# Eight experts on one core: the last result in a used buffer, stored by one DMA

## The chip, the cores and the metric

The kernel runs on 1 core of one Trainium2 chip. The time is device microseconds for the whole program, as the median of the runs. The profile is of one more execution with its own time; its span runs from the first to the last instruction, and all positions below are microseconds from the start of that span.

## The reference

For each of 8 experts there are 256 rows of 512 inputs, and two weight matrices. Everything comes in and goes out as 32-bit floats.

```
x (8, 256, 512)   w1 (8, 512, 2048)   w2 (8, 2048, 512)   b1 (8, 2048)   b2 (8, 512)
h   = max(x @ w1 + b1, 0)
out = h @ w2 + b2            # (8, 256, 512)
```

The weights of one expert are 4 MB each for w1 and w2, so the 8 experts read 64 MB of weights in all. One result is 512 KB.

## The kernel before

One expert is one stage. In stage s the kernel does the first product of expert s and the second product of expert s - 3 (`LAG = 3`), so there are 11 stages. TensorE transposes x (`transposes`, L101), makes 16 blocks of the hidden layer by 64 matmuls (`first_product`, L114), and for the second product adds the bias by a one-row matmul (L156) and then accumulates 32 matmuls into two PSUM tiles of 128 x 512 (`second_product`, L162). ScalarE applies the bias and the rectifier (L121).

The loads are issued by GpSimd, since they turn 32-bit floats into 16-bit ones on the way. They stand in a list called `ring`, whose order is fixed by hand: x and w1 of expert s, w2 of expert s - 3. `second_product` of the last expert reads its w2 from three pieces (`load_w2_piece`, L92), so that it can begin on the first. Those pieces are the last loads of the list.

The results of experts 0 to 6 are not stored when they are ready. `store` copies the two PSUM tiles into an SBUF tile `out`, one half by VectorE (L139) and one by ScalarE (L140), and remembers the tile in `pending`. `flush` (L135) issues the stores from GpSimd, behind all loads. The list ends with these flushes in the order of the experts, so the seven results lie in one DMA queue behind the last weights. Expert 5's result is stored in three parts by partition (`PARTS`): 25 partitions by SyncE (L145), 96 and 7 by GpSimd.

The result of expert 7 does not go into the list. VectorE copies one half, and SyncE stores that half (L148, 256 KB); ScalarE copies the other half and stores it itself (L149, 256 KB).

The tiles called `out` come from a pool of 8 buffers that go round. The first two hold the 32-bit x of experts 0 and 1 at the start, so the results of experts 0 to 5 take the other six buffers, and the results of experts 6 and 7 take the first two again. Those had been free since the first microseconds.

Of the kernel before, what the change touches and what calls it, by code (L numbers as in the profile page):

```python
# [11 lines left out]
def kernel(  # L12
# [9 lines left out]
    nc = tc.nc  # L22
    fp32 = mybir.dt.float32
    fp16 = mybir.dt.float16
    E, T, H = x.shape
    M = w1.shape[2]
    P = 128
    nTB = T // P
    nKC = H // P
    nJ = M // P  # L30
    LAG = 3
    LATE = range(E - 1)

    PARTS = {5: ((0, 25, True), (25, 121, False), (121, 128, False))}
# [9 lines left out]
    x_pool = ctx.enter_context(tc.tile_pool(name="xp", bufs=4))  # L46
    xT_pool = ctx.enter_context(tc.tile_pool(name="xTp", bufs=2))
    hT_pool = ctx.enter_context(tc.tile_pool(name="hT", bufs=LAG + 1))
    out_pool = ctx.enter_context(tc.tile_pool(name="outp", bufs=E))
    psum_x = ctx.enter_context(tc.tile_pool(name="psum_x", bufs=1, space=bass.MemoryType.PSUM))  # L50
    psum_h = ctx.enter_context(tc.tile_pool(name="psum_h", bufs=3, space=bass.MemoryType.PSUM))
    psum_o = ctx.enter_context(tc.tile_pool(name="psum_o", bufs=2, space=bass.MemoryType.PSUM))
# [10 lines left out]
    w1_sb = [None] * E  # L63
    w2_sb = [None] * E
    hT = [None] * E
    pending = {}

    def load_x(e):
# [66 lines left out]
                ordered(nc.gpsimd.dma_start(out=dst[p0:p1], in_=src[p0:p1]))  # L135

    def store(e, po):
        out_sb = out_pool.tile([P, nTB, H], fp32, tag="out", name="out")
        nc.vector.tensor_copy(out=out_sb[:, 0, :], in_=po[0])  # L139
        nc.scalar.copy(out=out_sb[:, 1, :], in_=po[1])  # L140
        dst = out[e].rearrange("(p tb) h -> p tb h", tb=nTB)
        if e < E - 1:
            for p0, p1, sync in PARTS.get(e, ()):
                if sync:
                    nc.sync.dma_start(out=dst[p0:p1], in_=out_sb[p0:p1])  # L145
            pending[e] = (dst, out_sb)
        else:
            nc.sync.dma_start(out=dst[:, 0, :], in_=out_sb[:, 0, :])  # L148
            nc.scalar.dma_start(out=dst[:, 1, :], in_=out_sb[:, 1, :])  # L149

    def second_product(e):
        po = []
        for tb in range(nTB):
            t = psum_o.tile([P, H], fp32, tag=f"po{tb}", name=f"po{tb}")
            po.append(t)
            ordered(nc.tensor.matmul(  # L156
                out=t, lhsT=ones1, rhs=b2_sb[0:1, e * H : (e + 1) * H], start=True, stop=False,
            ))
        for lo, hi, t in w2_sb[e]:
            for tb in range(nTB):  # L160
                for j in range(lo, hi):
                    ordered(nc.tensor.matmul(  # L162
                        out=po[tb],
                        lhsT=hT[e][:, j, tb * P : (tb + 1) * P],
                        rhs=t[:, j - lo, :],
                        start=False,
                        stop=(j == nJ - 1),
                    ))
        store(e, po)

    x32 = []
    for e in range(nXF32):
        x32.append(out_pool.tile([P, nTB, H], fp32, tag="out", name="x32"))
        (nc.sync if e == 0 else nc.scalar).dma_start(
            out=x32[e], max_dma_last_dim=2048, in_=x[e].rearrange("(p tb) h -> p tb h", tb=nTB)
# [4 lines left out]
        out=b2_sb,  # L180
        in_=b2.rearrange("e h -> (e h)").rearrange("(o f) -> o f", o=1),
# [10 lines left out]
    for j in range(nJ):  # L192
        for s in range(2):
            ordered(nc.tensor.matmul(  # L194
                out=pb[s * 64 : (s + 1) * 64, j, :, :],
# [5 lines left out]
    for s in range(2):  # L201
        nc.vector.tensor_copy(  # L202
            out=b1T[s * 64 : (s + 1) * 64, :, :], in_=pb[s * 64 : (s + 1) * 64, :, :, s]
# [13 lines left out]
    for lo, hi in ((0, 8), (8, 12), (12, 16)):  # L217
        ring.append((0, load_w2_piece, (E - 1, lo, hi)))
    for e in LATE:
        ring.append((e + LAG + 1, flush, (e,)))  # L220
# [40 lines left out]
```

## Time and profile before

| What | Value |
|---|---|
| median of 9 runs | 183.86 us (183.78 to 184.18) |
| the profiled execution's own time | 184.15 us |
| its span | 182.4 us |
| DMA, mean over the span | 222 GB/s on the SBUF side of the packets |
| HBM read and written | 71.39 MB and 4.19 MB, 414 GB/s over the span |
| TensorE busy | 135.7 us (74% of the span) |
| ScalarE busy | 62.6 us (34%) |
| GpSimd, VectorE busy | 20.1 us (11%), 13.2 us (7%) |

A load counts in the GB/s of the packets with the 16-bit size that arrives, so a stretch of loads at about 220 GB/s reads twice that from HBM. A stretch of stores moves 32-bit floats on both sides. The DMA row of the page gives the mean busy share of the core's 16 DMA engines in tenths for each of 40 slices of 4.56 us.

### The profile page before, as it was taken

To read this page: it belongs to the slowest core of one execution; us is meant where nothing else is said; L and a number is where in the kernel's file an instruction comes from. 1 tells how busy PE (TensorE), PEld (TensorE's weight loads), DVE (VectorE), ACT (ScalarE), POOL (GpSimd) and SP (SyncE) were. 2 spreads that over 40 slices of the span, in tenths; PEclk is the share of its full clock that TensorE was granted. 3 is DMA by queue.
4 is the path that set the end of the run, shared out by engine and by line. 5 is a ranking of instruction groups with operands and counts; after the bars stand their busy time and mean duration, and the time that the engine had idled before them with its cause. 6 is when DMAs were issued, how large, how long until landed. Compare 5 with 4: busy or idle time off the path is not lost.

```text
span 182.4 us, 2120 instructions
## 1 busy us (share of the span) xinstructions
PE 135.7 (74%) x912; PEld 94.6 (52%) x912; DVE 13.2 (7%) x21; ACT 62.6 (34%) x137; POOL 20.1 (11%) x43
## 2 busy tenths in 40 slices
PE   1805979479550999849980999849999999998700
PEld 1804979469540854845480754836489444433200
DVE  0410001001000101010100101010100101010100
ACT  0112679639560330924090330915059010100100
POOL 7200030300300010201010000200051011112100
PEclk9999999969998599999998599997999999999995
DMA  5999989998999999999999999999998999999992
GB/s 160 261 226 232 230 173 230 201 259 187 217 230 226 194 212 230 196 235 201 230 226 212 194 230 226 198 208 230 226 230 178 226 205 226 205 228 210 398 410 101
DMA packets 5687, 40.58 MB, mean 222 GB/s; under 512 B 654, under 2 KB 670, under 8 KB 3374
## 3 DMA queue, kind: packets, MB, share of 16 engines
q0 software_dynamic: 4784, 38.71, 96.3%
q1 hardware_dynamic: 446, 0.89, 1.4%
q10 hardware_dynamic: 448, 0.85, 1.4%
q8 instruction: 7, 0.11, 0.2%
q14 instruction: 2, 0.02, 0.0%
HBM read 71.39 MB, written 4.19 MB: 414 GB/s over the span
## 4 chain that ended last, share of the span: by engine, by line
DMA 68%; PE 24%; POOL 1%; issue 1%; ACT 0%; POOLq 0%
DMA x<-in_x_dram 44%; DMA w<-in_w_dram 16%; PE po L162 12%; PE ph L114 10%; DMA w1sb<-in_w_dram 8%; PE psx L101 1%; POOL w2sb L86 1%; PE po L156 1%; ACT out L140 0%; POOL w1sb L76 0%; POOLq L245 0%
## 5 line engine op out<-in xcount | busy, mean ns | idle before, releaser
L114 PE MATMUL ph<-xT,w1sb 128*128 128x256 f16 x512 | 67.7, 298 | 12.5 <-DMA w1sb<-in_w_dram 12.5
L121 ACT ACTIVATE hT<-ph,b1T 128x256 f16<-128x256 f32 x128 | 57.0, 474 | 44.6 <-PE ph L114 44.5
L114 PEld LDWEIGHTS <-w1sb 128*128 128x128 f16 x512 | 61.1, 148 | 18.3 <-DMA w1sb<-in_w_dram 13.4
L162 PE MATMUL po<-w2sb,hT 128*128 128x512 f16 x224 | 49.6, 379 | 0.0
L162 PEld LDWEIGHTS <-hT 128*128 128x128 f16 x256 | 24.5, 98 | 32.4 <-issue 4.1
L140 ACT COPY out<-po 128x512 f32<-128x512 f32 x8 | 4.7, 590 | 57.0 <-PE po L162 57.0
L101 PE MATMUL psx<-ident,x 128*128 128x128 f16 x64 | 6.2, 254 | 19.1 <-DMA x<-in_x_dram 18.4
L101 PEld LDWEIGHTS <-x 128*128 128x128 f16 x64 | 5.0, 124 | 20.1 <-DMA x<-in_x_dram 19.4
L76 POOL DMA_DIRECT2D w1sb<-in_w_dram x8 | 4.4, 555 | 64.9 <-PE ph L114 64.1
L107 DVE COPY xT<-psx 128x1024 f16<-128x1024 f16 x8 | 5.5, 692 | 83.3 <-PE psx L101 83.3
L86 POOL DMA_DIRECT2D w2sb<-in_w_dram x9 | 4.8, 536 | 55.3 <-PE po L162 55.3
L139 DVE COPY out<-po 128x512 f32<-128x512 f32 x8 | 5.5, 692 | 69.2 <-PE po L162 69.2
L162 PE MATMUL po<-w,hT 128*128 128x512 f16 x32 | 7.1, 379 | 0.7 <-DMA w<-in_w_dram 0.7
L135 POOL DMA_DIRECT2D out_dram<-out x8 | 4.3, 533 | 29.7 <-DVE out L139 8.7
L194 PE MATMUL pb<-ident,b_rows 16*64 16x16 f32 x64 | 3.7, 265 | 4.1 <-DMA b_rows<-in_b_dram 4.1
L194 PEld LDWEIGHTS pb<-ident,b_rows 16*64 16x64 f32 x64 | 3.6, 198 | 4.0 <-POOL ident masks.py:199 4.0
L156 PE MATMUL po<-b_sb,ones 1*128 1x512 f16 x16 | 4.8, 379 | 0.0
L121 ACT ACT_TABLE_LOAD x1 | 1.3, 1283 | 8.5 <-DVE b1T L202 8.5
L70 POOL DMA_DIRECT2D x<-in_x_dram x6 | 3.6, 598 | 0.7 <-DMA w1sb<-in_w_dram 0.7
L156 PEld LDWEIGHTS <-ones 1*128 1x128 f16 x16 | 0.9, 92 | 2.1 <-issue 2.1
L189 DVE CAST x<-x 128x1024 f16<-128x1024 f32 x2 | 1.4, 694 | 4.6 <-DMA x<-in_x_dram 4.6
L92 POOL DMA_DIRECT2D w<-in_w_dram x3 | 1.6, 557 | 0.0
(9 smaller groups left out, 2.6 us busy)
## 6 DMA issues: line engine op xcount, KB each, us to landing
w1sb<-in_w_dram POOLq DMA_DIRECT2D x8, 2048.0 KB, 33.8
w2sb<-in_w_dram POOLq DMA_DIRECT2D x5, 2048.0 KB, 46.6
w2sb<-in_w_dram POOLq DMA_DIRECT2D x4, 1024.0 KB, 28.0
out_dram<-out POOLq DMA_DIRECT2D x6, 512.0 KB, 21.1
x<-in_x_dram POOLq DMA_DIRECT2D x6, 256.0 KB, 39.3
w<-in_w_dram POOLq DMA_DIRECT2D x1, 1024.0 KB, 29.5
w<-in_w_dram POOLq DMA_DIRECT2D x2, 512.0 KB, 32.4
x<-in_x_dram SPq DMA_DIRECT2D x1, 512.0 KB, 4.2
```

The source lines that it names most:

```text
L76: ordered(nc.gpsimd.dma_start(out=w1_sb[e], in_=w1[e].rearrange("(p kc) m -> p kc m", kc=nKC)))
L86: ordered(nc.gpsimd.dma_start(out=t[:, lo : lo + step, :], in_=src[:, lo : lo + step, :]))
L101: ordered(nc.tensor.transpose(out=pt[:, kc, tb * P : (tb + 1) * P], in_=x16[e][:, tb, :].rearrange("p (q kc) -> p q kc", kc=nKC)[:, :, kc] ...
L107: nc.vector.tensor_copy(out=xT[e], in_=pt)
L114: ordered(nc.tensor.matmul(out=ph, lhsT=w1_sb[e][:, kc, :].rearrange("p (q j) -> p q j", j=nJ)[:, :, j], rhs=xT[e][:, kc, :], start=(kc == 0),
L121: nc.scalar.activation(out=hT[e][:, j, :], in_=ph, func=mybir.ActivationFunctionType.Relu, bias=b1T[:, j, e : e + 1], scale=1.0,)
L135: ordered(nc.gpsimd.dma_start(out=dst[p0:p1], in_=src[p0:p1]))
L139: nc.vector.tensor_copy(out=out_sb[:, 0, :], in_=po[0])
L140: nc.scalar.copy(out=out_sb[:, 1, :], in_=po[1])
L156: ordered(nc.tensor.matmul(out=t, lhsT=ones1, rhs=b2_sb[0:1, e * H : (e + 1) * H], start=True, stop=False,))
L162: ordered(nc.tensor.matmul(out=po[tb], lhsT=hT[e][:, j, tb * P : (tb + 1) * P], rhs=t[:, j - lo, :], start=False, stop=(j == nJ - 1),))
L194: ordered(nc.tensor.matmul(out=pb[s * 64 : (s + 1) * 64, j, :, :], lhsT=b1_rows.rearrange("r (q j) -> r q j", j=nJ)[:, :, j], rhs=ident[0 ...
```

## The change

The pool of `out` tiles has 7 buffers in place of 8. The results of experts 0 to 6 are kept in a list `results`, and expert 7's result goes into the tile of expert 4 (`REUSED = 4`). Its two copies therefore wait until the store of expert 4's result has been read out of that tile and has completed. The result is then stored by one SyncE DMA of 512 KB, and ScalarE issues no store. The positions of the first six results in the pool do not matter to anything else; experts 5 and 6 now take the two buffers that held x at the start.

```
-    out_pool = ctx.enter_context(tc.tile_pool(name="outp", bufs=E))
+    out_pool = ctx.enter_context(tc.tile_pool(name="outp", bufs=E - 1))
...
     def store(e, po):
-        out_sb = out_pool.tile([P, nTB, H], fp32, tag="out", name="out")
+        if e < E - 1:
+            results.append(out_pool.tile([P, nTB, H], fp32, tag="out", name="out"))
+        out_sb = results[e] if e < E - 1 else results[REUSED]
         nc.vector.tensor_copy(out=out_sb[:, 0, :], in_=po[0])
         nc.scalar.copy(out=out_sb[:, 1, :], in_=po[1])
         dst = out[e].rearrange("(p tb) h -> p tb h", tb=nTB)
-        if e < E - 1:
-            for p0, p1, sync in PARTS.get(e, ()):
-                if sync:
-                    nc.sync.dma_start(out=dst[p0:p1], in_=out_sb[p0:p1])
-            pending[e] = (dst, out_sb)
-        else:
-            nc.sync.dma_start(out=dst[:, 0, :], in_=out_sb[:, 0, :])
-            nc.scalar.dma_start(out=dst[:, 1, :], in_=out_sb[:, 1, :])
+        if e == E - 1:
+            nc.sync.dma_start(out=dst, in_=out_sb)
+            return
+        for p0, p1, sync in PARTS.get(e, ()):
+            if sync:
+                nc.sync.dma_start(out=dst[p0:p1], in_=out_sb[p0:p1])
+        pending[e] = (dst, out_sb)
```

No instruction changes its place on TensorE or GpSimd. On VectorE and ScalarE the last copy gains a wait on the DMA of expert 4's store. SyncE's last DMA is 128 x 1024 elements in place of 128 x 512 and waits for both copies; ScalarE's DMA behind its last copy is gone.

More of the change, by code (lines that the diff above doesn't have):

```diff
@@ L32 @@
     LATE = range(E - 1)
+    REUSED = 4
     PARTS = {5: ((0, 25, True), (25, 121, False), (121, 128, False))}
@@ L65 @@
     hT = [None] * E
+    results = []
     pending = {}
```

## The prediction

> **What bounds the kernel now.** I read the page's slices first, then the chain of waits, then the end of the span in finer windows.
>
> ```profile
> span 182.4 us, 2120 instructions
> ...
> DMA  5999989998999999999999999999998999999992
> GB/s 160 261 226 232 230 173 230 201 259 187 217 230 226 194 212 230 196 235 201 230 226 212 194 230 226 198 208 230 226 230 178 226 205 226 205 228 210 398 410 101
> ...
> q0 software_dynamic: 4784, 38.71, 96.3%
> ```
>
> The DMA engines are busy at nine tenths or more in nearly every slice, and 96.3% of that is GpSimd's queue q0. TensorE is busy for 74% and ends its last matmul at 172.1. From 169 on the rate stands near 400 GB/s: the loads are over and the stores drain. So the end is set by when the DMA engines have moved the last byte, and only the last 10 us are touched by the change. The chain of waits ends at the ScalarE copy (172.12 + 0.59) and does not follow the stores after it. The timeline of the end, and the times to landing, show what comes then:
>
> ```profile
> 160.58 0.53 POOL L135 DMA_DIRECT2D out_dram<-out  x1 [4.31 <-DMA w2sb<-in_w_dram]
> ...
> 170.47 0.55 POOL L135 DMA_DIRECT2D out_dram<-out  x1 [2.24 <-DMA w<-in_w_dram]
> 171.25 0.69 DVE L139 COPY out<-po 128x512 f32<-128x512 f32 x1 [8.51 <-PE po L162]
> 171.97 0.35 SPq L148 DMA_DIRECT2D out_dram<-out  x1
> 172.12 0.59 ACT L140 COPY out<-po 128x512 f32<-128x512 f32 x1 [7.75 <-PE po L162]
> 172.73 0.37 ACTq L149 DMA_DIRECT2D out_dram<-out  x1
> ```
>
> ```profile
> out_dram<-out SPq DMA_DIRECT2D x1, 256.0 KB, 6.6
> out_dram<-out ACTq DMA_DIRECT2D x1, 256.0 KB, 7.6
> ```
>
> The issue at 160.58 is expert 4's store (the fifth flush; asked for alone it lands 15.8 us later, at 176.4). The one at 170.47 is expert 6's; it lands after 9.6 us, at 180.1. Expert 7's halves land at 178.6 and 180.3. The last landing, 180.3, starts the end of the program, 2.1 us of waits and drains up to 182.4. Flushes 0 to 4 land some 1.3 us apart (30.0, 26.4, 22.9, 19.4 and 15.8 us after their issues at 141.16, 145.99, 150.84, 155.74 and 160.58), which is 512 KB at 419 GB/s.
>
> The DMA packets by queue, from 172 to 175.4, and the last stretches, with their DMA share and GB/s in the last two columns:
>
> ```profile
> DMA packets 384, 1.43 MB, mean 419 GB/s; under 512 B 37, under 2 KB 37, under 8 KB 383
> q0 software_dynamic: 383, 1.42, 101.9%
> q14 instruction: 1, 0.01, 0.6%
> ```
>
> ```profile
> 177.00:178.00 1.00, 0.00 (x0) 0.00 (x0) 0.00 (x0) 0.00 (x0) 0.00 (x0) 0.50 1.04 402
> 178.00:178.50 0.50, 0.00 (x0) 0.00 (x0) 0.00 (x0) 0.00 (x0) 0.00 (x0) 0.50 0.92 365
> 178.50:179.00 0.50, 0.00 (x0) 0.00 (x0) 0.00 (x0) 0.00 (x0) 0.00 (x0) 0.50 0.77 315
> 179.00:179.50 0.50, 0.00 (x0) 0.00 (x0) 0.00 (x0) 0.00 (x0) 0.00 (x0) 0.50 0.22 86
> 179.50:180.00 0.50, 0.00 (x0) 0.00 (x0) 0.00 (x0) 0.00 (x0) 0.00 (x0) 0.50 0.03 12
> ```
>
> The store issued by SyncE at 171.97 moves no packet up to 175.4: q1, SyncE's queue, is missing. Its first packet comes 3.5 us after the issue, and that of ScalarE's store 3.55 us after its own (packet records of the trace). The second block shows a ragged end. Adding up the shares from 178.0, all engines at full load would have ended at 178.97; a few run on to 179.77, and the last landing is 0.56 us behind that.
>
> **The change part by part.**
>
> *Removed: the early start.* Before, the halves are issued at 171.97 and 172.73. Now the copies wait for expert 4's landing. Nothing ahead of that landing changes in GpSimd's queue, and the SyncE packets began only at 175.47, so I leave it at 176.4. Had these packets held it up it would come some 0.2 us earlier: the nearest row against that is the spacing of 1.3 us from flush 3 to flush 4, as for the earlier ones. Waits on a DMA release TensorE here within 0.05 us (164.97 to 165.01).
>
> *Added: the wait.* VectorE's copy runs from 176.43 to 177.12 (0.69), ScalarE's beside it for 0.59. SyncE issues 0.03 later, as at 171.97 behind the copy's end at 171.94: 177.15. Behind the waiting copies nothing is queued: they are the last work of VectorE and ScalarE, and the DMA is SyncE's last. TensorE is done at 172.1, and the flushes of experts 5 and 6 are already issued at 165.56, 167.71 and 170.47. So the wait costs only what the late issue costs.
>
> *Moved: 512 KB behind the ring.* After flush 4 the ring holds 384 + 28 + 512 KB, 0.95 MB, which at 419 GB/s is 2.26 us. By bytes, the engines run dry of it at 178.97 - 1.25 = 177.7 on the mean. The latest one ends at 179.77 now; without its share of expert 7 (32 KB, eight packets of 4 KB, at an engine's 26 GB/s 1.25 us) at about 178.5. This is the cover: as long as the new store's packets are there by 177.7 to 178.5, the same bytes run through the same engines and nothing is lost.
>
> *How soon they are there* is the unknown. Bounds: at the start of the program, with the engines idle, the SyncE load of x at 0.74 has its first packet 1.08 us after its issue and ScalarE's load of b_rows 1.41 us. Under a full ring it is 3.5 us, as above. I take 1.3, since the ring is nearly empty when the store comes, and since ScalarE's second load at the start (x, issued at 1.22) began at 4.13, just as SyncE's was ending: a new queue seems to wait behind what the engines hold, and no longer. First packet 178.45; lowest 178.2, highest 180.65.
>
> The Trainium skill, "DMA: Bandwidth & Descriptors", section "Queues, rings and completion order", says that each engine goes round its queues packet by packet, so a new queue should not have to wait for another's ring to drain. The row disagrees: 2.2 to 2.4 us more than at the start, some fifteen 4 KB packets per engine. By the rule the latency would be the idle one, ring or not, and the likeliest sum below needs no luck; by the row alone it would be 3.5 us and the sum 186.0. I go with an explanation for both rows, a backlog that is gone at 178.
>
> *The transfer itself.* 512 KB at 419 GB/s is 1.25 us; the x load at the start took about 2.35 us from its first to its last packet, its first packets 0.6 us each. A store at the end of a draining ring is nearer to the stores, so I take 1.6. The landing comes 0.36 us (expert 6) to 0.56 us (expert 7) after the last packet; I take 0.5. Sum: 177.15 + 1.3 + 1.6 + 0.5 = 180.55, which is 3.4 us after issue. The x load as a whole, the one 512 KB DMA by SyncE in this trace, took 4.2 us.
>
> Against the change speaks a rule of the same page, section "Anatomy of one DMA — SWDGE (gpsimd) path": a DMA has a fixed part near 2.0 us, most of it the wait for the write to be confirmed (fitted for GpSimd's DMAs). Here it is paid twice in a row, for expert 4 and expert 7. The trace shows confirmations of 0.36 to 0.56 us, the first of which lies under the ring. The rule's 2.0 + 1.2 us would give an estimate of 180.35, hardly different from before; the rows give 180.55, and I keep them.
>
> *Edits at nothing.* ScalarE's DMA issue (0.37 us) goes away; at 172.73 it lay beside a drain of 7 us. Packets are 4 KB in place of 2 KB: from 176.2 to 178.1, with three queues mixed, the rate is 403 GB/s against 419, and 4% of 3 us is 0.12 us at most, a gain. One wait fewer stands at the end; these waits are under 0.03 us each. The smaller pool puts results 5 and 6 into buffers free since 7 us. If any of that cover is wrong the sizes stay under 0.2 us.
>
> *The sum.* The last landing goes from 180.3 to 180.55, +0.25 us on the span. The profiled execution took 184.15 (span 182.4 and 1.75 outside), 0.29 above the median, so I put the difference on the median: 183.86 + 0.25 = 184.1.
>
> **The rivals.**
>
> *The latency under load stays* (slower). Mechanism: the first packet of a SyncE store takes 3.5 us after its issue however little of the ring is left. Place: between 177.15 and 180.65, with the engines idle from 178.5. Then 180.65 + 1.25 + 0.5 = 182.4, +2.1, 186.0 us. It decides once the first packet is later than about 178.9. For it: all three hardware-queue stores here took 3.3 to 3.5 us, the 100 KB one at 156.85 too. Against it: the 1.08 and 1.41 us at the start.
>
> *The store starts cold* (slower). As the x load: 4.2 us from issue to landing, 181.35, +1.0, 184.9 us. For it: the only SyncE DMA of this size. Against it: that one read HBM with 64 KB of b_rows in between.
>
> *The drain becomes tidier* (faster). All engines start on the store with nothing else in the way: 1.08 + 1.25 + 0.36 from 177.15 is 179.85, -0.45, 183.4 us. For it: the ragged end, some 0.8 us in which most engines idle, and the 4% of mixed packets. Against it: the latest engine has the same bytes to move and ends near 179.7 anyway, so two things must go right.
>
> That the change does not do what it says I rule out: the copies could start at 171.25 and 172.12, and expert 4's store lands 4 us later, so the wait holds.
>
> **How the numbers follow.** A measurement of this kernel tells about 0.2%, 0.37 us, from no change: 183.49 to 184.23. The likeliest case, the overlap nearly complete, has 0.55, with its own range 183.6 to 184.55; of it 0.03 is faster, 0.36 the same and 0.16 slower. The cold start has 0.22 and the loaded latency 0.13, both slower. The tidier drain has 0.10, 0.09 faster and 0.01 the same. That makes faster 0.12, same 0.37, slower 0.51. Slower holds more than half, but split over three cases, so the predicted time is the likeliest case's, 184.1. The range 183.5 to 185.6 takes in that case, the cold start with 0.7 us beyond it and some of the tidier drain; it leaves out the loaded latency and the best of the faster case.
>
> **What would show it.** In the changed profile, VectorE's last copy should start near 176.4, released by a DMA, and SyncE's issue stand near 177.15. The first q1 packets are right at 178.2 to 178.6, wrong near 180. The DMA share should stay near 1 up to 177.5 and have at most a short dip before 179, no stretch of 1 us at nothing. The store should land 3.1 to 3.7 us after its issue. The prediction is wrong if that is over 4 us, or if expert 4's landing has moved by more than 0.3 us.

## The result: 0.65% faster, and the profile after

The changed kernel takes 182.69 us in the median of 10 runs (182.46 to 183.38), the kernel before 183.92 (31 runs, 183.77 to 184.24). The ratio is 0.9935, with a 95% interval of 0.9927 to 0.9943: 1.2 us faster. The forecast was 184.1 with a range of 183.5 to 185.6, so it had the wrong sign, and the measured time lies below the range.

The profiled execution took 182.66 us, with these lines on its page:

```profile
span 180.9 us, 2122 instructions
...
DMA  5999999999998999999999989999998999999995
GB/s 162 266 225 234 207 199 232 192 228 217 230 232 177 232 228 210 199 232 228 196 214 222 234 188 225 228 199 210 232 228 187 221 212 217 210 226 207 341 419 225
...
q0 software_dynamic: 4784, 38.71, 97.1%
```

The loads are as before, in bytes (q0's packets are the same) and in rate, near 220 GB/s. The difference is at the end. The timeline of the changed kernel:

```profile
170.51 0.55 POOL L137 DMA_DIRECT2D out_dram<-out  x1 [2.23 <-DMA w<-in_w_dram]
176.41 0.59 ACT L146 COPY out<-po 128x512 f32<-128x512 f32 x1 [11.45 <-DMA out_dram<-out]
176.43 0.69 DVE L145 COPY out<-po 128x512 f32<-128x512 f32 x1 [13.10 <-DMA out_dram<-out]
177.20 0.35 SPq L149 DMA_DIRECT2D out_dram<-out  x1
```

Up to SyncE's issue, things went as forecast: both copies are released by a DMA at 176.4, and SyncE issues at 177.20 (177.15 was forecast). After that it is quicker. The times to landing are these, first of SyncE's single store and then of expert 6's, the last that GpSimd issues:

```profile
out_dram<-out SPq DMA_DIRECT2D x1, 512.0 KB, 2.6
```

```profile
out_dram<-out POOLq DMA_DIRECT2D x1, 512.0 KB, 8.1
```

SyncE's store lands at 179.8 (before, the later half landed at 180.3). Expert 6's store is issued at the same time as before and lands at 178.6, where it was 180.1. The last stretches, with DMA share and GB/s at the right:

```profile
177.00:177.50 0.50, 0.00 (x0) 0.00 (x0) 0.12 (x1) 0.00 (x0) 0.00 (x0) 0.50 0.74 303
177.50:178.00 0.50, 0.00 (x0) 0.00 (x0) 0.00 (x0) 0.00 (x0) 0.00 (x0) 0.50 0.41 164
178.00:178.50 0.50, 0.00 (x0) 0.00 (x0) 0.00 (x0) 0.00 (x0) 0.00 (x0) 0.50 0.95 385
178.50:179.00 0.50, 0.00 (x0) 0.00 (x0) 0.00 (x0) 0.00 (x0) 0.00 (x0) 0.50 1.02 418
179.00:179.50 0.50, 0.00 (x0) 0.00 (x0) 0.00 (x0) 0.00 (x0) 0.00 (x0) 0.50 0.66 262
```

There is a dip between 177 and 178, in which the DMA engines run out of the ring's packets, and then SyncE's store almost alone. The dip costs 0.4 us of DMA time, and the kernel is faster all the same.

The last landing moved by 0.5 us and the span by 1.5. (The profiled execution of the kernel before was 0.2 us above its median, the changed one at its own; so the spans differ by somewhat more than the medians.) The other 1.0 us lies between the last landing and the end: 2.1 us before, 1.0 us now. What stands there are the closing instructions of the program. Among them are DRAINs: GpSimd stands at one for some 10 us here, until 1.5 us after its last DMA has landed. They are listed for the line that opens the kernel's context (count; duration in ns, least, median and longest; first and last start). Of the kernel before:

```profile
L256 POOLq DRAIN  x3: 46/98/10791, 170.8 to 182.1; - x3
L256 SPq DRAIN  x3: 7/7/7, 180.4 to 181.9; - x3
```

and of the changed kernel:

```profile
L261 POOLq DRAIN  x3: 46/98/9242, 170.8 to 180.6; - x3
L261 SPq DRAIN  x3: 7/7/7, 179.9 to 180.3; - x3
```

GpSimd's longest drain starts at 170.8, with its last DMA issue, and takes 10.79 us before and 9.24 us after. So it ends at 181.6 and at 180.1. SyncE, which waits for every landing, reaches its own drain at 180.4 before and 179.9 after. Before, then, SyncE was through at 180.5 and the program waited 1.1 us more for GpSimd. Now both are through within 0.1 us of each other. From GpSimd's drain to the end of the span it is 0.8 us in both.

### The profile page after: what moved, and what is told of

The parts are those of the page before. It is cut to its first block, busy times and chain, and to the rows that moved or that the text cites. A ratio compares the mean times of both kernels' runs of the same rounds, so it can differ in the third digit from the quotient of the medians.

```text
span 180.9 us, 2122 instructions
## 1 busy us (share of the span) xinstructions
PE 136.6 (76%) x912; PEld 94.9 (52%) x912; DVE 13.2 (7%) x21; ACT 62.8 (35%) x137; POOL 20.2 (11%) x43
## 4 chain that ended last, share of the span: by engine, by line
DMA 75%; PE 20%; issue 1%; POOL 1%; DVE 0%; POOLq 0%; DVEq 0%
DMA x<-in_x_dram 44%; DMA w2sb<-in_w_dram 14%; PE ph L116 10%; DMA out_dram<-out 8%; DMA w1sb<-in_w_dram 8%; PE po L167 8%; PE psx L103 1%; POOL w2sb L88 1%; PE po L161 1%; DVE out L145 0%; POOL w1sb L78 0%; DVEq L145 0%; POOLq L137 0%; POOLq L250 0%
## 5 line engine op out<-in xcount | busy, mean ns | idle before, releaser
L116 PE MATMUL ph<-xT,w1sb 128*128 128x256 f16 x512 | 68.8, 301 | 12.6 <-DMA w1sb<-in_w_dram 12.6
```

What stands on the lines that cost most here:

```text
L116: ordered(nc.tensor.matmul(out=ph, lhsT=w1_sb[e][:, kc, :].rearrange("p (q j) -> p q j", j=nJ)[:, :, j], rhs=xT[e][:, kc, :], start=(kc == 0),
```

## The experiments

Theory D: the end follows the later of two things, SyncE's wait for the last landing and GpSimd's drain, and the drain ends about 1.5 us after GpSimd's own last DMA has landed. The change helps because the last result no longer takes time of the DMA engines from GpSimd's queue while that queue empties. There are two rivals. In P, what saves is the single DMA with 4 KB packets, and without ScalarE's issue. In W, it is the wait as such. Ratios are to the kernel before, with 95% intervals.

**One DMA without the wait.** In the kernel before:

```
-            nc.sync.dma_start(out=dst[:, 0, :], in_=out_sb[:, 0, :])
-            nc.scalar.dma_start(out=dst[:, 1, :], in_=out_sb[:, 1, :])
+            nc.sync.dma_start(out=dst, in_=out_sb)
```

> The kernel before, with the last result in its own buffer and stored by one SyncE DMA of 512 KB behind both copies; no wait on the ring. Theory D (the program's end follows GpSimd's last drain, which ends about 1.4 us after GpSimd's last DMA has landed: 180.1 to 181.6 before, 178.6 to 180.0 after): the SyncE store is issued at about 172.75, shares the engines with the ring from about 176, expert 6's store still lands near 180, GpSimd's drain ends near 181.5: 183.6 to 184.1, no gain. Rival P (one DMA with 4 KB packets and without ScalarE's DMA is what saves): 182.6 to 183.1.

Measured: 183.82 us, ratio 0.9994 (0.9988 to 1.0001). Expert 6's store lands at 180.0, and GpSimd's drain ends at 181.5 (170.9 + 10.57):

```profile
L255 POOLq DRAIN  x3: 46/107/10568, 170.9 to 182.0; - x3
L255 SPq DRAIN  x3: 7/7/7, 180.3 to 181.7; - x3
```

P falls: the single DMA alone brings nothing that can be told from no change. The last result itself lands at 179.6 here, 0.7 us earlier than before, and the time stays.

**The wait with two halves.** In the changed kernel, the edit above the other way round.

> The changed kernel, with expert 4's buffer and its wait kept, but stored as two halves by SyncE and ScalarE as before. Theory D: GpSimd's queue is empty by 178.3 as in the changed kernel, its drain ends near 180.0, the halves land near 179.8: 182.5 to 182.9, the gain is kept. Rival P: the gain falls away, at least half of it: 183.2 to 184.

Measured: 182.73 us, 0.9927 (0.9914 to 0.9939). The drain ends at 180.1. With the wait the whole gain is there, whichever way the result is stored.

**A slice of the last result by GpSimd.** In the changed kernel:

```
-            nc.sync.dma_start(out=dst, in_=out_sb)
+            nc.sync.dma_start(out=dst[0:112], in_=out_sb[0:112])
+            nc.gpsimd.dma_start(out=dst[112:128], in_=out_sb[112:128])
```

> The changed kernel, but the last 16 of the 128 partitions of the last result (64 KB of 512 KB) are stored by GpSimd, behind the same copies. Bytes and the time of the last landing stay nearly the same (within 0.3 us). Theory D: GpSimd's last DMA now lands near 179.7 in place of 178.6, its drain ends near 181.1: span 182.0, 183.6 to 184.0, the gain is gone. Rival P, and any theory by which only the last landing counts: 182.5 to 183.0.

Measured: 184.71 us, 1.0035 (1.0023 to 1.0048), slower than the kernel before. The expectation missed by 0.7 us: GpSimd issues only at 177.62 and its 64 KB need 3.0 us, so the last landing is at 180.6 and not near 179.7. So this run moved two things, the last landing and the drain. The drain sets the end (the longest takes 4532 ns from 177.6 to 182.1, and SyncE is at its own by 181.0):

```profile
L262 POOLq DRAIN  x3: 46/98/4532, 177.6 to 182.6; - x3
L262 SPq DRAIN  x3: 7/7/7, 181.0 to 182.4; - x3
```

**One kilobyte by GpSimd.** This moves the drain and leaves the stores alone. In the changed kernel:

```
+    spare = singles.tile([16, 16], fp32)
...
             nc.sync.dma_start(out=dst, in_=out_sb)
+            nc.gpsimd.dma_start(out=spare, in_=out_sb[0:16, 1, 0:16])
```

> The changed kernel, and behind ScalarE's last copy GpSimd moves 1 KB (16 partitions of 16 numbers) from the last result to an unused SBUF tile. Nothing waits for it and no store changes, so SyncE's last landing stays near 179.8. Theory D: the 1 KB is issued near 177.1 to 177.6 and lands 2.3 to 3 us later (64 KB took 3.0 us in the run with GpSimd's slice), GpSimd's drain ends 1.5 us behind it, at 181 to 181.9: span 181.8 to 182.7, 183.5 to 184.5, the whole gain gone by 1 KB. Any theory in which only the moving of the results counts: 182.5 to 182.9.

Measured: 184.11 us, 1.0011 (1.0005 to 1.0018). The landings, and the drains behind them:

```profile
out_dram<-out SPq DMA_DIRECT2D x1, 512.0 KB, 2.7
...
spare<-out POOLq DMA_DIRECT2D x1, 1.0 KB, 2.8
```

```profile
L263 POOLq DRAIN  x3: 46/107/4303, 177.2 to 182.0; - x3
L263 SPq DRAIN  x3: 7/7/7, 180.3 to 181.7; - x3
```

SyncE's store is issued at 177.11 and lands at 179.8, as in the changed kernel. The kilobyte is issued at 177.20 and lands at 180.0. The drain ends at 181.5, and the gain is gone. This is the cleanest evidence for D: nothing waits for the kilobyte but the end of the program, and the last landing of all comes only 0.13 us later than in the changed kernel (179.96 against 179.83), while the time is 1.4 us longer.

**Waiting for the last store of the ring.** `REUSED = 6` in the changed kernel.

> The changed kernel with REUSED = 6: the copies wait for expert 6's store, the last of the ring. With the changed kernel's own durations: landing 178.6, copies to 179.35, SyncE issue 179.4, first packet 0.85 later, 1.42 us of packets, landing 182.0, and 1.1 us to the end: span 183.1, 184.6 to 185.2. Theory D: GpSimd's drain ends near 180.0 all the same, 2 us before the last landing, since it follows GpSimd's own DMAs. If the drain followed the last landing of any queue, it would end near 183.4 and the time be 186 or more.

Measured: 184.77 us, 1.0045 (1.0030 to 1.0059), within the 184.6 to 185.2 worked out from the changed kernel's durations. GpSimd's drain still ends at 180.1 (170.9 + 9.19), 2 us before SyncE's last landing at 182.1. So the drain follows GpSimd's own DMAs, and not the last landing of any queue.

**Waiting for expert 5.** `REUSED = 5`.

> The changed kernel with REUSED = 5: the copies wait for expert 5's three stores, the last of which lands at 177.3 there. Issue near 178.15, first packet 0.85 later, 1.42 us of packets, landing 180.75, then 0.95 us from the last landing to the end as in the run with REUSED = 6: span 181.7, 183.3 to 183.7. GpSimd's drain ends near 180.1 and no longer counts. If the end were still the drain's, 182.7.

Measured: 183.77 us, 0.9992 (0.9983 to 1.0000): no gain left, 0.1 us above the expectation's upper end. Expert 5's three stores release the copies at 177.7, 0.3 us later than worked out. The drain ends at 180.2, and SyncE's landing, at 181.1, sets the end.

**Waiting for expert 3.** `REUSED = 3`.

> The changed kernel with REUSED = 3: expert 3's store lands at 175.1, so the SyncE store is issued near 175.95, 1.25 us earlier, with 1.8 us of the ring left. Theory B (a new queue waits behind what the engines hold already): first packets near 177.7, the ring is not held up, expert 6's store lands at 178.6 as in the changed kernel, the drain ends at 180.1: 182.6 to 182.8, no gain since the drain sets the end. Rival R (the engines go round the queues packet by packet at once): first packet 0.85 us after issue, at 176.8, the ring shares from there and ends 0.5 to 1 us later, the drain with it: 183.2 to 183.7.

Measured: 182.65 us, 0.9933 (0.9920 to 0.9945), equal to the changed kernel. SyncE issues at 176.07, 1.1 us earlier. From 176 to 177:

```profile
q0 software_dynamic: 128, 0.39, 95.4%
q1 hardware_dynamic: 3, 0.01, 3.0%
```

The first SyncE packet comes 0.86 us after its issue, as rival R has it. But only 3 of SyncE's packets stand in this stretch and 12 in the next half microsecond, perhaps on engines that are through with the ring (which engine a packet ran on is not in the trace, so this is not shown). Expert 6's store lands at 178.6, not held up, and the time is theory B's.

**Waiting for expert 2.** `REUSED = 2`.

> The changed kernel with REUSED = 2: expert 2's store lands at 173.7, issue near 174.5, with 3.2 us of the ring left. Theory B with a backlog of at most 3.5 us: first packets at 177.4 to 178, time within 0.4 us of the changed kernel, 182.7 to 183.1. Rival R: first packets at 175.4, as in the kernel before, ring and drain late as there: 183.6 to 184.

Measured: 183.0 us, 0.9952 (0.9938 to 0.9966), within B's range. The first packet comes 2.24 us after the issue, at 176.7, which is 0.7 us before the earliest that B gave. Expert 6's store lands at 179.1 and the drain ends at 180.6, half a microsecond later than in the changed kernel: here the ring is held up. Of the five places tried (experts 2 to 6), 3 and 4 are the best, and 2 and 5 lose on either side.

**The ring's last store moved, without any wait.** In the kernel before:

```
-    LATE = range(E - 1)
+    LATE = range(E - 2)
...
-            nc.sync.dma_start(out=dst[:, 0, :], in_=out_sb[:, 0, :])
+            ordered(nc.sync.dma_start(out=dst[:, 0, :], in_=out_sb[:, 0, :]))
+            d6, s6 = pending.pop(e - 1)
+            ordered(nc.sync.dma_start(out=d6, in_=s6))
```

> The kernel before, without any wait on a buffer; only expert 6's result is taken off GpSimd's list and stored by SyncE in one DMA behind its half of the last result, issued near 172.4. Bytes are the same. Theory D: GpSimd's queue ends with expert 5's result, landing before 178, its drain before 179.5; then the last SyncE or ScalarE landing, near 180.0, sets the end with 0.95 us: span 180.9 to 181.2, 182.6 to 183.0, most of the gain without the wait. Rival W (the wait, which keeps the last store out of the ring, is what saves): 183.7 to 184.1 as before.

Measured: 182.98 us, 0.9948 (0.9935 to 0.9961). W falls: most of the gain is there without a wait on a buffer, and with the results in the buffers of the kernel before. The closing lines:

```profile
L258 POOLq DRAIN  x3: 46/164/12517, 167.7 to 181.2; - x3
L258 SPq DRAIN  x3: 7/7/7, 180.2 to 180.9; - x3
```

The time was forecast, but not quite the way to it: GpSimd's last landing is at 178.8 and not before 178, its drain ends at 180.2 and not before 179.5, and SyncE is through at 180.3. Here the span ends 1.2 us after that, where the other kernels need 0.8. In the records of the trace nearly all of these 0.4 us lie between two closing semaphore instructions of GpSimd; its cause stays open.

**Two attempts at a faster one.** With `REUSED = 3`, half of expert 6's result goes from GpSimd to SyncE, behind the last result. First partitions 64 to 127 (`PARTS` leaves 0 to 63 to GpSimd):

```
+            late = out[e - 1].rearrange("(p tb) h -> p tb h", tb=nTB)
+            ordered(nc.sync.dma_start(out=late[64:128], in_=results[e - 1][64:128]))
```

> An attempt at a version that beats both: REUSED = 3, and of expert 6's result GpSimd stores only partitions 0 to 63; SyncE stores the other 64 (256 KB) behind its store of the last result. If the end is the later of GpSimd's drain (1.5 us after its last landing) and SyncE's last landing with its waits (0.95 us before the end): GpSimd's queue runs dry 0.6 us earlier, drain ends near 179.5; SyncE's 768 KB start near 177.2 and land near 179.6: span 180.5 to 180.7, 182.3 to 182.5, 0.2 to 0.4 below the changed kernel. If the end has another cause: 182.7 or more.

Measured: 182.64 us, 0.9933 (0.9920 to 0.9945), no better than the changed kernel and above the 182.3 to 182.5 that the theory gave. The drain ends at 179.5 as meant, but SyncE's last landing slips to 180.0:

```profile
178.50:179.00 0.50, 0.00 (x0) 0.00 (x0) 0.00 (x0) 0.00 (x0) 0.00 (x0) 0.50 0.96 287
179.00:179.50 0.50, 0.00 (x0) 0.00 (x0) 0.00 (x0) 0.00 (x0) 0.00 (x0) 0.50 0.81 213
```

The DMA engines are busy and move little. Then the second row block of all partitions in place of the half of the partitions (`late[:, 1, :]`):

> The second attempt at a version that beats both, as the first (REUSED = 3, half of expert 6's result stored by SyncE behind the last result) but the half is the second of the two row blocks of all 128 partitions, 2 KB each, and not partitions 64 to 127. In the first attempt GpSimd's drain ended at 179.5 as wanted, but from 178.5 on the engines showed 0.8 to 0.96 of busy share with 213 to 287 GB/s, and SyncE's last landing was at 180.0. If that came from reading one half of the partitions, all SyncE packets end near 179.3 and land near 179.6, span 180.4 to 180.6: 182.2 to 182.4. If it came from SyncE's queue carrying 768 KB at all, the landing is at 180 again: 182.6 to 182.8.

Measured: 182.76 us, 0.9929 (0.9915 to 0.9942). From 178.5 to 179.0 the rate is back at 393 GB/s with a share of 1.00, so the low rate goes with storing half of the partitions (the packets also went from 4 KB to 2 KB, so this is not the only difference). But a few packets end as late as 179.7, where most are through by 179.3, and SyncE's last landing is at 180.1: the second case of the expectation. Neither run beats the changed kernel clearly; with the drain off the path, SyncE's last landing takes over at the same place.

All 13 kernels side by side, in us: GpSimd's last landing (issue plus time to landing), the end of its long drain, the time at which SyncE is through with its waits and its own drain, and the end of the span.

| Kernel | last GpSimd landing | drain ends | between | SyncE through | span ends |
|---|---|---|---|---|---|
| before | 180.1 | 181.6 | 1.5 | 180.5 | 182.4 |
| one DMA, no wait | 180.0 | 181.5 | 1.5 | 180.4 | 182.3 |
| changed (expert 4) | 178.6 | 180.1 | 1.5 | 180.0 | 180.9 |
| two halves with the wait | 178.6 | 180.1 | 1.5 | 180.0 | 180.9 |
| expert 2 | 179.1 | 180.6 | 1.5 | 180.5 | 181.4 |
| expert 3 | 178.6 | 180.1 | 1.5 | 179.9 | 180.8 |
| expert 5 | 178.7 | 180.2 | 1.5 | 181.2 | 182.0 |
| expert 6 | 178.6 | 180.1 | 1.5 | 182.2 | 183.0 |
| 1 KB by GpSimd | 180.0 | 181.5 | 1.5 | 180.4 | 182.3 |
| 64 KB by GpSimd | 180.6 | 182.1 | 1.5 | 181.0 | 182.9 |
| expert 6 by SyncE | 178.8 | 180.2 | 1.4 | 180.3 | 181.5 |
| half of 6, by partitions | 178.0 | 179.5 | 1.5 | 180.1 | 180.9 |
| half of 6, by row blocks | 178.2 | 179.7 | 1.5 | 180.2 | 181.0 |

In every row but that of expert 6 by SyncE, the span ends 0.8 us after the later of the drain and SyncE, whichever of the two it is. The pairs that share a drain but not SyncE's time (expert 4 and expert 6), and those that nearly share SyncE's time but not the drain (half of 6 by row blocks and 1 KB by GpSimd), show that each of the two can set the end.

## Why the prediction was wrong

- *The step that failed is the first reading of the end*: "The last landing, 180.3, starts the end of the program, 2.1 us of waits and drains up to 182.4". Those 2.1 us were taken as fixed behind whichever landing is last. They were not: 1.1 us of them was GpSimd's drain behind expert 6's store, which landed 0.2 us earlier than the last half. Fixed are the 1.5 us from GpSimd's own last landing to the end of its drain, and, but for one run with 1.2, the 0.8 us from the later of the two finishes to the end of the span. The closing lines shown above were in the profile before, with a drain of 10.79 us in them, and the prediction read past them.
- *What the cover does for the queue it covers* was not carried on. The prediction worked out that GpSimd's queue would be dry by 177.7 to 178.5 (its last packet ends at 178.2) and used that only as the time up to which SyncE's store may come late. That expert 6's store then lands 1.5 us sooner was in the same number, and this was the gain.
- *The sum of the store* was mis-sized: 3.4 us from issue to landing, measured 2.6. The first packet came 0.85 us after its issue (1.3 taken, 1.08 as the lowest), the packets took 1.43 us (1.6), and the landing followed 0.35 us behind the last one (0.5). The cold start did not happen. The cover was not free, though: the first packet came at 178.05, between 177.7 and 178.5, and the dip still cost 0.4 us. With 2.6 us and the fixed tail the sum would have been 183.3, below the range too, but with about half of the gain.
- *The latency under load* was in the main read rightly. It is not fixed: 3.5 us under a full ring (before; also 3.5 in the run with one DMA and no wait), 2.24 with expert 2, and 0.85 with experts 3 to 6. The backlog explanation, chosen over the packet-by-packet rule, fits the times of the runs with experts 2 and 3, but not their first packets: with expert 2 they came 0.7 us before its earliest, and with expert 3 three came 0.86 us after the issue. What the latency depends on stays open.
- *Two readings* were off, without weight for the sum: the 96.3% is q0's share of the time of all 16 engines, not of their busy time; and of the x load's first twelve packets four took 0.54 to 0.68 us and the others 0.17 to 0.27, not 0.6 each.
- *The wait's own steps* were right to 0.1 us: landing at 176.4, copies, issue at 177.2, nothing queued behind them.
- *The rivals.* "The drain becomes tidier" had the right sign, with a chance of 0.10, and gave 183.4. That nearness is luck: its mechanism (engines with nothing else in the way, fewer mixed packets) is not what saved, as two runs show, that with one DMA and no wait and that with two halves and the wait.

## What to carry to other kernels

An end that is bound by transfers can have more than one finish line: here SyncE's wait for the landings, and GpSimd's drain 1.5 us behind the last landing of GpSimd's own DMAs. So try to let the queue with the longer finish run empty first and put the last bytes on the other one, even if the DMA engines idle for a moment in between, as here. Read the closing instructions by engine before you take a tail as fixed, and work out how a change moves the landing of every queue, not only of the last transfer.

## What the runs showed of the hardware

- GpSimd's closing drain ended 1.4 to 1.5 us after its last DMA landed in all 13 kernels, for 512 KB as for 1 KB, whatever the other queues did. Why it takes that long no run shows.
- A 1 KB copy issued by GpSimd took 2.8 us to land beside SyncE's 512 KB, which took 2.7. Its first packet came 2.1 us after the issue, and the landing 0.5 us behind its last.
- A SyncE store of 512 KB that meets a nearly empty set of engines was 2.6 us from issue to landing; the same store issued into a full ring took 6.8 us (one DMA, no wait).
- With a 256 KB store of partitions 64 to 127 under way, beside the end of another store, the DMA engines were 0.81 to 0.96 busy and moved 213 to 287 GB/s. With the same bytes stored from all partitions it was 393 GB/s at 1.00. In the records, 4 KB packets took 0.16 us in the changed kernel's store; here 47 of SyncE's 106 from 178 on took over 0.18, up to 0.35.
